# Storing one output tile in five pieces, so that one DMA engine moves fewer rows

## The chip, the cores and the metric

The kernel runs on one core of a Trainium2 chip. A core has TensorE (PE), VectorE (DVE), ScalarE (ACT), GpSimd (POOL) and SyncE (SP), and sixteen DMA engines that move data between HBM and SBUF. The metric is the time of one execution on the device in microseconds (us), as a median of several runs.

## The reference

Batched products of two tensors, over 96 independent pairs of matrices:

```python
batch, n_heads, seq_t, seq_s, channels = 8, 12, 512, 512, 64
x = randn(batch, n_heads, seq_t, channels)   # float32
y = randn(batch, n_heads, seq_s, channels)
out = np.einsum('bhtc,bhsc->bhts', x, y).astype(np.float32)
```

The inputs are 12.6 MB each, the output is 100.7 MB of float32. Four fifths of the traffic is output.

## The kernel before

**Work.** The 96 matrix pairs are taken in 6 groups of 16, loaded as one x tile and one y tile of 128 partitions x 4096 float32 (2 MB) each. The inputs are cast to bf16 and kept (`xk`, `yb`), x is mixed into `xb` by copies, and both are turned on VectorE (`xT`, `yT`). The output is made in 24 tiles, `t` = 0 to 23, of 128 partitions x 8192 float32 (4 MB). A tile is made in four quarters: eight matmuls fill a PSUM tile `pm` (L212), and ScalarE copies it to a quarter of an SBUF slot (L114).

**Slots and stores.** There are three slots of 4 MB, used for loads at first and for output tiles afterwards. When all four quarters of a tile are in its slot, SyncE issues one store (L233): `nc.sync.dma_start(ov[i, z], slots[s])`. The view `ov` has, for one tile, 64 row pairs `p`, two rows `u` in each, and 8192 elements:

```python
ov = out.rearrange("b h t s -> (b h t s)").rearrange(
    "(i u z p n) -> i z p u n", u=2, z=2, p=P // 2, n=K * S
)
```

So one SBUF partition is one row of the store, a contiguous run of 32 KB in HBM. A store has 128 rows. ScalarE refills a slot only when the store that reads it has landed. The last five tiles use slots 2, 1, 0, 2, 1, so that the slot of tile 21 (slot 0) isn't filled again.

**Order.** Everything stands in one order, written out by hand at the end of the function. `emit` records what an instruction reads and writes, and `need` (L72 to L85) puts the semaphore waits that follow from that in front of it, on its engine (L82). A DMA names the semaphore that it raises by 16 (`dma=`). Each engine carries out its own instructions in order. SyncE issues all the DMAs; GpSimd issues none, and has nothing to do after the last y tile is cast. The function ends with SyncE waiting for the last store of each slot:

```python
need("sp", [(f"dma{i}", ticks[f"dma{i}"]) for i in range(0, 2 * BIG, 2)])
```

After it come the barriers of all engines that end the program.

Of the kernel before, what the change touches and what calls it, by code (L numbers as in the profile page):

```python
# [9 lines left out]
def kernel(  # L10
# [22 lines left out]
    nc = tc.nc  # L33
    B, H, T, C = x.shape
    _, _, S, _ = y.shape
    P = 128
# [8 lines left out]
    D = 32  # L45
    BIG = 3
    NT = 2 * NH
    fp32 = mybir.dt.float32
    bf16 = mybir.dt.bfloat16
    u32 = mybir.dt.uint32  # L50
# [3 lines left out]
    xv = x.rearrange("b h t c -> (b h t c)").rearrange("(g p n) -> g p n", p=P, n=R * C)  # L54
    yv = y.rearrange("b h t c -> (b h t c)").rearrange("(g p n) -> g p n", p=P, n=R * C)
    ov = out.rearrange("b h t s -> (b h t s)").rearrange(
        "(i u z p n) -> i z p u n", u=2, z=2, p=P // 2, n=K * S
    )

    sb = ctx.enter_context(tc.tile_pool(name="sb", bufs=1))  # L60
    ps = ctx.enter_context(tc.tile_pool(name="ps", bufs=1, space=bass.MemoryType.PSUM))
    slots = [sb.tile([P, K * S], fp32, name=f"slot{i}") for i in range(BIG)]
    xks = [sb.tile([P, R, C], bf16, name=f"xk{i}") for i in range(NG - 1)]
    ybs = [sb.tile([P, R // 2 * D], u32, name=f"yb{i}") for i in range(2 * NG - 3)]
    xb = sb.tile([P, K * E * D], u32, name="xb")
    xTs = [sb.tile([P, K * D * E], u32, name=f"xT{i}") for i in range(2)]
    yTs = [sb.tile([P, D * R // 2], u32, name=f"yT{i}") for i in range(2)]
    pms = [ps.tile([P, 4, S], fp32, name=f"pm{i}") for i in range(2)]
    engines = {"act": nc.scalar, "dve": nc.vector, "pool": nc.gpsimd, "pe": nc.tensor, "sp": nc.sync}
    sems, ticks, known, snaps, writer, readers = {}, {}, {e: {} for e in engines}, {}, {}, {}  # L70

    def need(name, points):  # L72

        best = {}
        for p, v in points:
            if known[name].get(p, 0) < v:
                best[p] = max(best.get(p, 0), v)
        for p, v in list(best.items()):
            if any(snaps[q, w].get(p, 0) >= v for q, w in best.items() if q != p):
                del best[p]  # L80
        for p, v in best.items():
            engines[name].wait_ge(sems[p], v)  # L82
            known[name][p] = v
            for q, w in snaps[p, v].items():
                known[name][q] = max(known[name].get(q, 0), w)  # L85

    def emit(name, make, reads=(), writes=(), dma=None):

        points = [writer[r] for r in (*reads, *writes) if r in writer]
        points += [v for w in writes for v in readers.get(w, ())]  # L90
        if name == "pool" and name in ticks:
            points.append((name, ticks[name]))
        need(name, points)
        p, step = (name, 1) if dma is None else (f"dma{dma}", 16)
        if p not in sems:
            sems[p] = tc.alloc_semaphore(p)
        make().then_inc(sems[p], step)
        at = (p, ticks.get(p, 0) + step)
        ticks[p] = at[1]
        snaps[at] = {**known[name], p: at[1]}  # L100
        if dma is None:
            snaps[at][name] = at[1]
        for r in reads:
            readers.setdefault(r, []).append(at)
        for w in writes:
            writer[w], readers[w] = at, []
# [14 lines left out]
    def load(n, place):  # L121
        where[n] = place
        s, half = divmod(place, 2)
        emit(
            "sp",
            lambda: nc.sync.dma_start(
                slots[s][:, half * R * C:(half + 1) * R * C], (yv if n % 2 else xv)[n // 2]
            ),
            writes=[("slot", s, 2 * half), ("slot", s, 2 * half + 1)],
            dma=place,  # L130
        )
# [5 lines left out]
    def keep_x(n):  # L137
        src, reads = held(n)
        xk = n // 2 % len(xks)
        copy("act", xks[xk].rearrange("p r c -> p (r c)"), src, reads, [("xk", xk)])  # L140
# [7 lines left out]
    def keep_y(n, half):  # L148
        src, reads = held(n)
        ys = src.rearrange("p (r c) -> p r c", c=C)  # L150
        b = home(n // 2, half)
        yv2 = ybs[b].bitcast(bf16).rearrange("p (j c w) -> p j w c", j=R // 2, w=2)
        for ch in range(2):
            copy(
                in_front[2 * half + ch],
                yv2[ch * 64:(ch + 1) * 64],
                ys[half * 64:(half + 1) * 64, :, ch * D:(ch + 1) * D].rearrange(
                    "p (j w) c -> p j w c", w=2
                ),
                reads,  # L160
                [("yb", b, ch)],
            )

    def mix(i, name, parts=range(4)):

        g, half = divmod(i, 2)
        xk = g % len(xks)
        xv2 = xb.bitcast(bf16).rearrange("p (k e c u) -> p k e c u", k=K, e=E, u=2)
        for part in parts:
            ch, u = divmod(part, 2)  # L170
            lo = half * 64 + u * D
            copy(
                name,
                xv2[part * D:(part + 1) * D, :, :, :, u],
                xks[xk][lo:lo + D, :, ch * D:(ch + 1) * D].rearrange("p (e k) c -> p k e c", k=K),
                [("xk", xk)],
                [("xb", part)],
            )

    def turn_x(i):  # L180
        half = i % 2
        emit(
            "dve",
            lambda: nc.vector.transpose(  # L184
                xTs[half].rearrange("p (k r e) -> p k e r", k=K, e=E),
                xb.rearrange("p (k e c) -> p k e c", k=K, e=E),
            ),
            [("xb", part) for part in range(4)],
            [("xT", half)],
        )  # L190

    def turn_y(i):
        g, half = divmod(i, 2)
        b = home(g, half)
        emit(
            "dve",
            lambda: nc.vector.transpose(  # L197
                yTs[half].rearrange("p (r j) -> p j r", r=D),
                ybs[b].rearrange("p (j c) -> p j c", c=D),
            ),  # L200
            [("yb", b, ch) for ch in range(2)],
            [("yT", half)],
        )
# [24 lines left out]

    def store(t, s):
        i, z = divmod(t, 2)  # L230
        emit(
            "sp",
            lambda: nc.sync.dma_start(ov[i, z], slots[s]),  # L233
            reads=[("slot", s, part) for part in range(4)],
            dma=2 * s,
        )

    with tc.tile_critical():  # L238
        for n in range(2 * BIG):
            load(n, n)  # L240
        emit(
            "dve",
            lambda: nc.vector.memset(xb, 0.0),  # L243
            writes=[("xb", part) for part in range(4)],
        )
        keep_x(0)
        mix(0, "dve")
        turn_x(0)
        keep_y(1, 0)
        keep_y(1, 1)  # L250
        turn_y(0)
        keep_x(2)
        load(6, 2)
        mix(1, "pool", range(1))
        keep_y(3, 0)
        keep_y(3, 1)
        load(7, 3)
        mix(1, "pool", range(1, 3))
        mix(1, "dve", range(3, 4))
        keep_x(4)  # L260
        load(8, 4)
        quarter(0, 0, 0, "act")
        keep_y(5, 0)
        keep_y(5, 1)
        load(9, 5)
        turn_x(1)
        quarter(0, 0, 4, "act")
        keep_x(6)
        load(10, 2)
        quarter(0, 0, 8, "act")  # L270
        keep_y(7, 0)
        keep_y(7, 1)
        load(11, 3)
        turn_y(1)
        quarter(0, 0, 12, "act")
        store(0, 0)
        mix(2, "pool", range(2))
        keep_x(8)
        quarter(1, 2, 0, "act")
        keep_y(9, 0)  # L280
        keep_y(9, 1)
        mix(2, "pool", range(2, 4))
        quarter(1, 2, 4, "act")
        keep_x(10)
        quarter(1, 2, 8, "act")
        quarter(1, 2, 12, "act")
        store(1, 2)
        keep_y(11, 0)
        turn_y(2)
        quarter(2, 1, 0, "act")  # L290
        quarter(2, 1, 4, "act")
        keep_y(11, 1)
        quarter(2, 1, 8, "act")
        quarter(2, 1, 12, "act")
        store(2, 1)
        turn_x(2)
        mix(3, "dve")
        for t in range(3, NT):
            s = (0, 2, 1)[t % 3]
            for k in range(0, K, 4):  # L300
                quarter(t, s, k, "act")
            store(t, s)
            i = t // 2 + 2
            if t % 2 and i < NH:
                turn_y(i)
                turn_x(i)
                if i + 1 < NH:
                    mix(i + 1, "dve")
        need("sp", [(f"dma{i}", ticks[f"dma{i}"]) for i in range(0, 2 * BIG, 2)])


# [28 lines left out]
```

## Time and profile before

| | |
|---|---|
| median of 3 runs | 301.94 us (301.93 to 302.73) |
| profiled execution, its own time | 302.08 us |
| span of the profiled execution, first to last instruction | 300.3 us |
| busy: ACT, DVE, PE, POOL | 71%, 52%, 48%, 14% of the span |
| DMA | 125.95 MB, mean 419 GB/s over the span |
| stores: 24 of 4096 KB | 21.9 us from issue to landing (median) |

The profiled execution's time is 1.78 us more than its span. In the profile, SPq is SyncE's own queue of instructions, L12 is line 12 of the kernel, and all times count from the span's start. A window's DMA share and GB/s count each packet where it starts, with its whole size and length, so that a share can be over 1.

### The profile page before, as it was taken

Reading aid. Unit: us, or ns where it says so; the run is one execution under the profiler, and the core shown is the slowest. Engines: PE = TensorE matmul, PEld = TensorE weight load, DVE = VectorE, ACT = ScalarE, POOL = GpSimd, SP = SyncE. Lnnn points to the kernel's source line nnn. Section 1 sums busy time; section 2 is a strip of 40 time slices with the busy share of each in tenths; the row PEclk is TensorE's granted clock in tenths of the full one; section 3 lists DMA queues with packets and bytes.
Section 4 is the critical chain, followed back from the end, with each engine's and each line's share of the span. In section 5 each row is a group of like instructions: output and inputs, shape, how many; then the busy total and the mean of one; then the engine's idle time right before and its main releaser. Section 6 shows DMA issues by size and latency. Waiting matters only on the chain.

```text
span 300.3 us, 1880 instructions
## 1 busy us (share of the span) xinstructions
PE 144.7 (48%) x768; PEld 46.5 (15%) x768; DVE 156.8 (52%) x78; ACT 212.8 (71%) x109; POOL 41.9 (14%) x17
## 2 busy tenths in 40 slices
PE   0000633454864767655753575558664754664000
PEld 0000210111211222121211121112211211211000
DVE  2399999859494862927709349087192510000000
ACT  1665999999997669776876678667966696669000
POOL 0117977990000000000000000000000000000000
PEclk9999955559598675778779877776679778775555
DMA  7999999999999999999999999999999999999992
GB/s 275 426 436 430 421 419 430 439 421 417 419 445 454 423 417 428 443 445 428 417 428 445 445 423 423 426 445 450 419 423 426 441 450 419 423 426 441 450 423 118
DMA packets 5192, 125.95 MB, mean 419 GB/s; under 512 B 576, under 2 KB 576, under 8 KB 576
## 3 DMA queue, kind: packets, MB, share of 16 engines
q1 hardware_dynamic: 5184, 125.83, 97.9%
q8 instruction: 6, 0.10, 0.1%
q14 instruction: 2, 0.02, 0.0%
HBM read 25.17 MB, written 100.66 MB: 419 GB/s over the span
## 4 chain that ended last, share of the span: by engine, by line
DMA 52%; ACT 19%; DVE 14%; PE 5%; issue 2%; ACTq 0%; SPq 0%
DMA out_dram<-slot 49%; ACT slot L114 16%; DVE yb L116 8%; PE pm L212 5%; DVE xb L116 4%; DMA slot<-in_x_dram 3%; ACT xk L114 2%; DVE yT L197 1%; DVE xT L184 1%; ACT yb L114 1%; ACTq L82 0%; SPq L335 0%; SPq L238 0%
## 5 line engine op out<-in xcount | busy, mean ns | idle before, releaser
L114 ACT ACTIVATE slot<-pm 128x2048 f32<-128x2048 f32 x96 | 175.1, 1877 | 49.3 <-DMA out_dram<-slot 43.3
L212 PE MATMUL pm<-yT,xT 128*64 128x512 bf16 x768 | 144.7, 526 | 130.8 <-ACT slot L114 100.1
L212 PEld LDWEIGHTS pm<-yT,xT 128*64 128x64 bf16 x768 | 46.5, 139 | 228.2 <-ACT slot L114 151.9
L116 DVE COPY xb<-xk 32x2048 bf16<-32x2048 bf16 x41 | 59.5, 1451 | 10.6 <-ACT xk L114 9.3
L197 DVE STREAM_TRANSPOSE yT<-yb 128x1024 uint32<-128x1024 uint32 x12 | 23.6, 1969 | 68.2 <-PE pm L212 68.1
L184 DVE STREAM_TRANSPOSE xT<-xb 128x2048 uint32<-128x2048 uint32 x12 | 46.2, 3848 | 0.1
L116 DVE CAST yb<-slot 64x2048 bf16<-64x2048 f32 x12 | 27.9, 2321 | 4.6 <-DMA slot<-in_y_dram 4.3
L114 ACT ACTIVATE xk<-slot 128x4096 bf16<-128x4096 f32 x6 | 21.7, 3617 | 11.6 <-DMA slot<-in_x_dram 11.6
L116 POOL COPY xb<-xk 32x2048 bf16<-32x2048 bf16 x7 | 22.9, 3272 | 9.7 <-DVE xT L184 9.4
L116 POOL CAST yb<-slot 64x2048 bf16<-64x2048 f32 x6 | 18.8, 3138 | 15.8 <-DMA slot<-in_y_dram 15.3
L114 ACT ACTIVATE yb<-slot 64x2048 bf16<-64x2048 f32 x6 | 14.8, 2474 | 2.8 <-DMA slot<-in_y_dram 2.5
L243 DVE MEMSET xb<- 128x2048 uint32 x1 | 1.8, 1765 | 1.4 <-SPq L238 1.4
L114 ACT ACT_TABLE_LOAD x1 | 1.3, 1283 | 0.9 <-SPq L238 0.9
L324 POOL MEMSET const-float32-0.0<- 128x1 f32 x1 | 0.1, 98 | 0.2 <-issue 0.2
L324 POOL MEMSET const-bfloat16-1.0<- 128x1 bf16 x1 | 0.1, 101 | 0.0
L324 POOL MEMSET const-float32-1.0<- 128x1 f32 x1 | 0.1, 98 | 0.0
L324 POOL MEMSET const-uint8-127<- 128x1 uint8 x1 | 0.1, 98 | 0.0
## 6 DMA issues: line engine op xcount, KB each, us to landing
out_dram<-slot SPq DMA_DIRECT2D x24, 4096.0 KB, 21.9
slot<-in_x_dram SPq DMA_DIRECT2D x6, 2048.0 KB, 14.8
slot<-in_y_dram SPq DMA_DIRECT2D x6, 2048.0 KB, 11.8
```

What stands on the lines that cost most here:

```text
L114: lambda: nc.scalar.activation(dst, src, COPY)
L116: else engines[name].tensor_copy(dst, src),
L184: lambda: nc.vector.transpose(xTs[half].rearrange("p (k r e) -> p k e r", k=K, e=E), xb.rearrange("p (k e c) -> p k e c", k=K, e=E),),
L197: lambda: nc.vector.transpose(yTs[half].rearrange("p (r j) -> p j r", r=D), ybs[b].rearrange("p (j c) -> p j c", c=D),),
L212: last = nc.tensor.matmul(pms[pm][w * 64:(w + 1) * 64, j, :], xT[:, k + j, h, :], yT[:, h * S:(h + 1) * S], start=True, stop=True,)
L243: lambda: nc.vector.memset(xb, 0.0),
L324: nc = _bacc.Bacc("TRN2", target_bir_lowering=False, num_devices=1)
```

## The change

Tile 21, the last but two (`UNEVEN = NT - 3`), is no longer stored by one DMA but by five. SyncE issues a store of rows 0 to 95, two of four rows each (every second row of 118 to 125) and one of the last two rows. GpSimd issues a store of rows 96 to 117, and ahead of it a small load of ten runs of 64 bytes into a new tile `spare` that nothing reads. Each of the six DMAs has a semaphore of its own. At the end SyncE waits for all DMAs but the last store, and ScalarE waits for that one. All other tiles, all loads and all arithmetic are as before.

```diff
+    UNEVEN = NT - 3
...
+    spare = sb.tile([P, 16], fp32, name="spare")
...
     def store(t, s):
         i, z = divmod(t, 2)
+        if t == UNEVEN:
+            return store_unevenly(t, s)
         emit(
...
+    def store_unevenly(t, s):
+
+        i, z = divmod(t, 2)
+        runs = P // 2
+        some = 3 * runs // 4
+        most = some + 11
+        pieces = [("sp", slice(0, 2 * some), ov[i, z][:some])]
+        pieces.append(("pool", slice(2 * some, 2 * most), ov[i, z][some:most]))
+        for u in range(2):
+            pieces.append(("sp", slice(2 * most + u, 2 * runs - 2, 2), ov[i, z][most:runs - 1, u]))
+        pieces.append(("sp", slice(2 * runs - 2, 2 * runs), ov[i, z][runs - 1]))
+        for n, (name, rows, dst) in enumerate(pieces):
+            if name == "pool":
+                emit(
+                    "pool",
+                    lambda: nc.gpsimd.dma_start(spare[:10, :16], xv[0][:15, :16].rearrange("(a b) n -> a b n", b=3)[:, :2]),
+                    writes=["spare"],
+                    dma=100,
+                )
+            emit(
+                name,
+                lambda: engines[name].dma_start(dst, slots[s][rows]),
+                reads=[("slot", s, part) for part in range(4)],
+                dma=101 + n,
+            )
...
-        need("sp", [(f"dma{i}", ticks[f"dma{i}"]) for i in range(0, 2 * BIG, 2)])
+        last = f"dma{2 * s}"
+        need("sp", [(p, n) for p, n in ticks.items() if p.startswith("dma") and p != last])
+        need("act", [(last, ticks[last])])
```

## The prediction

> **What bounds the kernel now.** I read the page first.
>
> ```profile
> DMA  7999999999999999999999999999999999999992
> DMA packets 5192, 125.95 MB, mean 419 GB/s; under 512 B 576, under 2 KB 576, under 8 KB 576
> q1 hardware_dynamic: 5184, 125.83, 97.9%
> q8 instruction: 6, 0.10, 0.1%
> ```
>
> Sixteen DMA engines are busy from the first slice to the last but one, and no compute engine is above 71%. Only the rows left to move count. Next I asked who waits for whom from 245 us on (us in total, times, longest), and what the chain of waits is there (start, us, what).
>
> ```profile
> ACT slot L114 <- DMA out_dram<-slot: 7.0, 3, 2.3
> ```
>
> ```profile
> 247.87 21.94 DMA out_dram<-slot
> ...
> 273.78 3.65 ACT slot L114 x2
> ```
>
> ScalarE waits for a store to free its slot, refills it by 277.4 us and is done; from there the last stores drain. Then I cut the tail into windows (the last two columns are DMA share and GB/s).
>
> ```profile
> 293.00:294.00 1.00, 0.00 (x0) 0.00 (x0) 0.00 (x0) 0.00 (x0) 0.00 (x0) 0.50 1.14 492
> 294.00:295.00 1.00, 0.00 (x0) 0.00 (x0) 0.00 (x0) 0.00 (x0) 0.00 (x0) 0.50 0.69 295
> 295.00:296.00 1.00, 0.00 (x0) 0.00 (x0) 0.00 (x0) 0.00 (x0) 0.00 (x0) 0.50 0.00 0
> 296.00:297.00 1.00, 0.00 (x0) 0.00 (x0) 0.00 (x0) 0.00 (x0) 0.00 (x0) 0.50 0.08 33
> 297.00:298.00 1.00, 0.00 (x0) 0.00 (x0) 0.00 (x0) 0.00 (x0) 0.00 (x0) 0.50 0.08 33
> 298.00:299.00 1.00, 0.00 (x0) 0.00 (x0) 0.00 (x0) 0.00 (x0) 0.00 (x0) 0.50 0.00 0
> ```
>
> 33 GB/s in 1 us is 33 KB: one row starts in 296 to 297 and one in 297 to 298, with nothing beside them. One engine moves its last two rows alone. The trace's packet records (start, length and size of each) say the same to 10 ns. A row takes 1.213 us. Joined end to start they make sixteen chains, and the last rows end at 294.43 to 294.91 (seven engines), 295.37, 295.58, 295.78 to 296.21 (six), and **298.45** (one). The last landing is at 298.92, the span ends at 300.3.
>
> Why that engine is late also stands there. Between 72 and 279 us some 150 rows, about 15 in every 20 us, which is one engine's share, take some 25 ns over 1.213; in sum 3.9 us. The six engines at 295.8 to 296.2 each served one of the six 16 KB instruction fetches of the page (a gap of 0.85 to 0.95 us and a next row longer by 0.37 to 0.41). The records don't number the engines; that the late one is the change's "engine 4" I can't see.
>
> **The change part by part.**
>
> *The rows.* Rows 0 to 95 are six for each of sixteen engines. Rows 96 to 117 by GpSimd are two for each of eleven, 4 + 4 are two for each of four, the last two are one for each of two. If the eleven are 5 to 15, the four 0 to 3 and the two 0 and 1, engine 4 has 6 rows where it had 8, engines 0 and 1 have 9, and the rest 8. The late engine then ends at 298.45 - 2 x 1.213 - 2 x 0.025 = 295.97. Engines 0 and 1, if of the early seven, end at 294.9 + 1.21 = 296.1 at most. What is late next is the six fetch engines, at 296.21. So the end moves by 298.45 - 296.21 = **2.24 us**.
>
> [...]
>
> *Issue.* SyncE issues four DMAs where it issued one. A store's issue takes 0.54 us (median of L233), so at most 3 x 0.54 = 1.6 us more, at 257.7 us. Behind it stands the store of tile 22, issued at 267.7 when ScalarE has filled its slot: 8 us of cover, cost 0. Without cover it would be 1.6 us. GpSimd's last operation ends at 67.7 us; nothing is queued behind its DMAs and nothing but the end waits for them. Its generation has no row here: between SyncE's 0.33 us and GpSimd's own 3.4 us casts. Even 3.4 us is off the path, since rows 96 to 117 have from 258 to 286 us.
>
> *Jumping the queue.* GpSimd's rows come by another queue and may go ahead of tile 20's rows on eleven engines, which can then land 2 x 1.213 = 2.43 us later than 269.8. ScalarE refills that slot for tile 23, so its last store would be issued at 279.9, not 277.4. The first engines need it when tile 22 is moved, about 285.1 (its first landing); a DMA starts moving 1.0 us after its issue (the first load: 0.96 to 1.98). About 4 us of cover are left, cost 0.
>
> *A foreign queue between rows.* The price of a switch is read from the instruction fetches: 16 KB cost an engine 0.88 + 0.40 = 1.28 us, and the 8 KB one at 122.9 us 0.30 + 0.35 = 0.65. Proportional to bytes: 2 x 0.65 - 1.28 leaves 0.02 us for a switch. But at twice a store's time per byte (32 KB in 1.213 is 0.61 for 16 KB). So two rows by GpSimd cost 0 if they run as SyncE's do, and 2 x 1.3 = 2.6 us if they run as fetches do, on engines that would then end last. They are 32 KB rows from SBUF to HBM, as the stores are, so I take 0.
>
> *The last wait.* After its wait, at 298.92, SyncE signals all engines (299.16), they answer (299.20 to 299.25), and the barriers run to 300.3. With ScalarE waiting, SyncE has signalled long before, and ScalarE's answer is the only one missing. Nothing is queued behind ScalarE's wait; its last copy ended at 277.4. The hop is worth 0.2 us at most; a wait that ScalarE takes longer to leave costs as much. Bounds -0.2 to +0.2, value -0.1, since the hop is there in the records.
>
> *Sum.* 302.08 - 2.24 - 0.1 = 299.74 for the profiled execution, which is 0.14 above the median: **299.6 us**, 0.8% less.
>
> **The rivals.** A measurement can tell about 0.3% here, 0.9 us.
>
> *One extra row in the wrong place (0.10).* If engine 0 or 1 is one of the six fetch engines, its ninth row ends at 296.21 + 1.21 = 297.42, and the gain is 1.03 + 0.1: 300.8 us. For it: six of the fifteen others are fetch engines. Against: the seven early ones are the largest group, and the fetches fall on six different engines, which looks like a run of neighbours.
>
> *The rows don't fall as meant (0.12).* If GpSimd's 22 rows are dealt to the first eleven engines, engine 4 keeps 8 rows, and engines 0 and 1 have 11: 294.9 + 3 x 1.21 = 298.5, where the late one is. Or the late engine is another one. Either way 301.9, bounds 301.6 to 302.2: no change.
>
> *The partial tiles are read slower (0.22, the slower side).* All 36 DMAs of the trace have 128 rows, one for each partition. None shows what a transfer from 96 partitions costs. If rows that engines read together share a path, a row takes up to 2 x 1.213. Each doubled row on an engine costs 1.21, so the gain of 2.34 is gone at two of its six; with three the time is 301.94 - 2.34 + 3.64 = 303.2, with all six 306.9. For it: one row at a time takes exactly 1.213 on fifteen engines, which is a hard limit of something, and the packets at the start of the first load, where all engines begin at once, took up to 1.97 us for 16 KB instead of 0.61. Against: the engines drift by up to 3.9 us, three rows, against each other while the stores go on, so which rows are read together changes, and 1.213 doesn't.
>
> [...]
>
> **How the numbers follow.** Forecast 0.56, extra row 0.10, no effect 0.12, partial tiles 0.22. Faster by over 0.3% is the first two, 0.66; within 0.3% is 0.12; slower 0.22. Below, the forecast reaches 299.0: 299.6 less the other 0.1 of the hop and half a row (0.6) that the order of fetches may give. Above, the range takes in the extra row, no effect and the partial tiles up to three doubled rows, 303.2; beyond are some 0.15 above and 0.03 below. The likeliest case alone has 299.0 to 300.2.
>
> **What would show it.** Right: in windows of 1 us from the end back, no stretch with 33 GB/s alone, the last landing 2.3 us earlier against the span's start, the DMA share at 1.0 through 258 to 275 us. Of the steps: the copies of tile 23 still end before 280 us; tile 22's store is issued at about 267.7. Wrong: two single rows are still left at the end (placement), one single row (the extra row), or the DMA rate between 258 and 275 us falls under 420 GB/s and ScalarE's wait for tile 20's slot grows by over 2.4 us (partial tiles).

## The result: slower, and the profile after

The changed kernel takes 310.12 us (median of 6 runs, 309.39 to 310.49), the kernel before 302.23 us beside it (6 runs). The ratio is 1.026, 95% interval 1.0245 to 1.0274: **7.9 us slower**. The profiled execution took 309.94 us, with a span of 308.2. The forecast was 299.6, in a range up to 303.2.

The page after, its GB/s slices and queues:

```profile
GB/s 272 434 432 427 417 432 430 410 430 453 417 425 447 425 436 435 418 459 417 419 451 425 421 447 419 442 438 417 455 419 425 447 421 425 387 291 311 425 379 68
DMA packets 5260, 125.95 MB, mean 409 GB/s; under 512 B 644, under 2 KB 644, under 8 KB 644
q1 hardware_dynamic: 5172, 125.11, 96.6%
q0 software_dynamic: 80, 0.72, 0.8%
```

The bytes are the same. Up to the thirty-fourth slice the rate is as before; then come 387, 291 and 311 GB/s, which is from 262 us on, when tile 21 moves. The page's DMA issues (size, time from issue to landing) show the pieces:

```profile
out_dram<-slot SPq DMA_DIRECT2D x1, 3072.0 KB, 27.3
out_dram<-slot POOLq DMA_DIRECT2D x1, 704.0 KB, 15.3
```

The first piece has three quarters of a tile and needs 27.3 us where a whole tile needs 21.9. The waits from 245 us on and the chain of waits:

```profile
ACT slot L116 <- DMA out_dram<-slot: 11.4, 3, 6.7
```

```profile
247.86 26.35 DMA out_dram<-slot
...
278.18 3.65 ACT slot L116 x2
```

Tile 20's store, already under way, lands 4.4 us later than before (26.35 for 21.94), and ScalarE's longest wait grows from 2.3 to 6.7 us. The same stretch in windows, first of the kernel before, then of the changed one (DMA share and GB/s are the last two columns):

```profile
264.00:279.00 15.00, 7.78 (x40) 2.36 (x36) 0.00 (x0) 10.59 (x6) 0.00 (x0) 0.61 1.01 434
279.00:282.00 3.00, 0.00 (x0) 0.00 (x0) 0.00 (x0) 0.00 (x0) 0.00 (x0) 0.50 1.01 437
```

```profile
264.00:279.00 15.00, 7.08 (x38) 2.33 (x36) 0.00 (x0) 7.77 (x5) 0.00 (x0) 0.61 1.05 324
279.00:282.00 3.00, 0.91 (x6) 0.03 (x2) 0.00 (x0) 2.83 (x2) 0.00 (x0) 0.50 0.79 240
...
303.00:304.00 1.00, 0.00 (x0) 0.00 (x0) 0.00 (x0) 0.00 (x0) 0.00 (x0) 0.50 0.15 66
304.00:305.00 1.00, 0.00 (x0) 0.00 (x0) 0.00 (x0) 0.00 (x0) 0.00 (x0) 0.50 0.15 66
305.00:306.00 1.00, 0.00 (x0) 0.00 (x0) 0.00 (x0) 0.00 (x0) 0.00 (x0) 0.50 0.08 33
```

This is the pair to read: a share of 1.05 with 324 GB/s. The engines aren't idle; the same rows take longer. In the packet records 88 rows that start between 261.9 and 285.1 us take between 1.31 and 5.2 us instead of 1.213. Their excess sums to 94 us, 5.9 us for each engine. The 0.79 of the second stretch isn't idle time either: it comes from counting each row where it starts, and by the records all sixteen engines are at work without a gap from 264 to 297 us. The prediction named these signs for its partial tiles: a rate under 420 GB/s, and ScalarE's wait longer by over 2.4 us (here 4.4). And the end is no longer one late engine but a long tail: the last store's sixteen landings lie between 298.2 and 307.0 us. Their mean moved by 5.95 us (295.86 to 301.81), and the last one's distance from the mean by 2.1 (3.06 to 5.19). Together that is the 8.1 us by which the last landing moved.

### The profile page after: what moved, and what is told of

Read it like the earlier page. It is cut to its first block, busy times and chain, and to the rows that moved or that the text cites. A ratio compares the mean times of both kernels' runs of the same rounds, so it can differ in the third digit from the quotient of the medians.

```text
span 308.2 us, 1888 instructions
## 1 busy us (share of the span) xinstructions
PE 143.1 (46%) x768; PEld 46.2 (15%) x768; DVE 156.3 (51%) x78; ACT 212.7 (69%) x109; POOL 43.6 (14%) x19
## 4 chain that ended last, share of the span: by engine, by line
DMA 52%; ACT 18%; DVE 14%; PE 5%; issue 2%; ACTq 0%; SPq 0%
DMA out_dram<-slot 49%; ACT slot L116 15%; DVE yb L118 8%; PE pm L214 5%; DVE xb L118 4%; DMA slot<-in_x_dram 3%; ACT xk L116 2%; DVE yT L199 1%; DVE xT L186 1%; ACT yb L116 1%; ACTq L84 0%; SPq L367 0%; SPq L268 0%
## 5 line engine op out<-in xcount | busy, mean ns | idle before, releaser
L214 PE MATMUL pm<-yT,xT 128*64 128x512 bf16 x768 | 143.1, 521 | 136.9 <-ACT slot L116 106.2
L118 DVE COPY xb<-xk 32x2048 bf16<-32x2048 bf16 x41 | 58.6, 1430 | 10.5 <-ACT xk L116 9.3
L257 POOL DMA_DIRECT2D spare<-in_x_dram x1 | 1.0, 965 | 0.3 <-POOL yb L118 0.3
## 6 DMA issues: line engine op xcount, KB each, us to landing
out_dram<-slot SPq DMA_DIRECT2D x23, 4096.0 KB, 21.9
out_dram<-slot SPq DMA_DIRECT2D x1, 3072.0 KB, 27.3
```

The costliest lines, as they stand in the source:

```text
L118: else engines[name].tensor_copy(dst, src),
L214: last = nc.tensor.matmul(pms[pm][w * 64:(w + 1) * 64, j, :], xT[:, k + j, h, :], yT[:, h * S:(h + 1) * S], start=True, stop=True,)
L257: lambda: nc.gpsimd.dma_start(spare[:10, :16], xv[0][:15, :16].rearrange("(a b) n -> a b n", b=3)[:, :2]),
```

## Experiments

The main theory from here on is the slower rival of the prediction, called the *crowded path* in the texts below: rows that engines read together from neighbouring partitions share one row's rate. That is a supposition: the paths and groups of partitions in those texts belong to it, and no run shows which partitions would share, or what. Its rivals are GpSimd's queue, the number and size of the pieces, and the wait at the end. All experiments are edits of the kernel before; `pieces` replaces the store of tile 21 as in the change, and unless said otherwise the wait at the end stays with SyncE.

**Two halves by columns, two halves by partitions.**

```diff
+h = K * S // 2
+pieces = [("sp", slots[s][:, q * h:(q + 1) * h], ov[i, z][:, :, q * h:(q + 1) * h]) for q in range(2)]
```

> Tile 21 is stored by two SyncE transfers of all 128 partitions, each with half of the columns (16 KB rows). [...] GpSimd's queue as the cause: no change. Number and size of pieces as the cause (7.9 us for five pieces more): some 1.5 to 2 us slower.

```diff
+pieces = [("sp", slots[s][64 * q:64 * q + 64], ov[i, z][32 * q:32 * q + 32]) for q in range(2)]
```

> Tile 21 is stored by two SyncE transfers of 64 partitions each, all columns, 32 KB rows as before. Crowded path: sixteen engines read 64 rows that lie on half of the paths, each row takes 2 x 1.213 = 2.43 us, the tile 19.4 us instead of 9.7: about 9.7 us slower, 312 us, rows of 2.4 us in the trace. GpSimd's queue: no change, 302.2. Number of pieces: as for the two pieces of columns, at most 2 us slower.

Columns: 302.13 us against 302.09, ratio 0.9999 (0.9989 to 1.0008). Partitions: 310.54 us, ratio 1.0283 (1.0237 to 1.0329), 8.4 us slower. Same bytes, same number of pieces, both by SyncE. The stretch in windows, columns first, then partitions:

```profile
264.00:279.00 15.00, 7.42 (x42) 2.19 (x40) 0.00 (x0) 11.05 (x6) 0.00 (x0) 0.84 0.99 421
```

```profile
264.00:279.00 15.00, 7.65 (x44) 2.35 (x40) 0.00 (x0) 11.19 (x7) 0.00 (x0) 0.84 1.04 281
279.00:282.00 3.00, 0.00 (x0) 0.00 (x0) 0.00 (x0) 0.00 (x0) 0.00 (x0) 0.53 0.97 218
```

218 GB/s at a share of 0.97 is half of the 437 of the kernel before in the same window; the windows of 3 us on either side of it have 229 and 240. In the partition run 111 rows take between 1.32 and 4.44 us, and 42 of them 2.546 to 2.549: 2.1 times one row's time, as if two engines shared one path, with 25.7 GB/s between them where one alone has 27.0. The records don't show which engines meet. By the run of columns, two pieces and rows of half the size cost nothing.

**Rows 0 to 95 and 96 to 127.**

```diff
+pieces = [("sp", slots[s][:96], ov[i, z][:48]), ("sp", slots[s][96:], ov[i, z][48:])]
```

> Tile 21 is stored by two SyncE transfers, rows 0 to 95 and rows 96 to 127; no GpSimd, no small pieces, and the wait at the end stays with SyncE. Crowded path: most of the changed kernel's loss of 7.9 us is there, 306 to 312 us, and rows of 1.8 to 4 us. GpSimd's queue or the small pieces: no change, 302.2 us.

312.31 us, ratio 1.0345 (1.0322 to 1.0368): 10.2 us slower, just above the upper end of what the crowded path gave. The same stretch in a window:

```profile
264.00:279.00 15.00, 7.54 (x40) 2.22 (x36) 0.00 (x0) 9.33 (x6) 0.00 (x0) 0.61 1.07 333
```

Again the share is full and the rate is three quarters; 86 rows take 1.29 to 4.9 us, 89 us over 1.213 in sum. GpSimd, the pieces of four rows and ScalarE's wait aren't needed for the loss.

**The whole tile by GpSimd.**

```diff
+pieces = [("pool", slots[s], ov[i, z])]
```

> Tile 21 is stored by one GpSimd transfer of all 128 rows; everything else goes as before. Crowded path: each engine keeps its own partitions, so 302.2 us within 1 (GpSimd's rows go beside SyncE's, the sum of rows is the same). GpSimd's queue as the cause: several us slower; the changed kernel had two rows of eight there on eleven engines and lost 7.9 us, so four times as many rows would lose well over 8.

302.28 us, ratio 1.0003 (0.9994 to 1.0012). All 128 rows by GpSimd, going beside SyncE's, cost nothing, and 121 of the 128 take 1.213 us exactly. Tile 20's store lands 7.6 us later than in the kernel before (277.4 for 269.8), so GpSimd's rows do go in between its rows, and that is covered too.

**Even and odd partitions.**

```diff
+pieces = [("sp", slots[s][u:128:2], ov[i, z][:, u]) for u in range(2)]
```

> Tile 21 is stored by two SyncE transfers of 64 rows, the even and the odd partitions. Each reaches all groups of partitions, where the two halves of the run before reached half of them each. [...] Crowded path with each engine kept to its own group whatever the transfer: no change, 302.1 us.

302.32 us, ratio 1.0003 (0.9994 to 1.0012). Again two SyncE transfers of 64 rows of 32 KB, and no loss:

```profile
264.00:279.00 15.00, 8.57 (x40) 2.54 (x40) 0.00 (x0) 10.88 (x6) 0.00 (x0) 0.61 0.99 427
```

Against the halves, only which partitions stand in one transfer differs, and with them which rows of HBM it writes: 427 GB/s for 281. So it is neither 64 rows nor two transfers that cost, but 64 *neighbouring* partitions. Whether the rows meet in SBUF, where they are read, or in HBM, where they are written, no run separates. If the crowded path holds, no change here means that each engine keeps to partitions of its own in this transfer too. A loss of 5 to 10 us, which I had also held possible, isn't there. How rows are dealt to the engines, these runs don't show.

**Which engine is late.**

```diff
+for n, k in enumerate((1, 2, 4, 5, 10)):
+    emit("sp", lambda: nc.sync.dma_start(spares[n][:k, :16], xv[0][:3 * k:3, :16]),
+         writes=[("spare", n)], dma=101 + n)
```

> Behind the last store SyncE issues fifteen tiny loads of 2, 3, ... 16 rows of 64 bytes, so that each one's landings show when that many engines have come to the end of their rows. If a transfer of k rows uses the k lowest engines and the late engine is number 4: the loads of 2, 3 and 4 rows land 1 us or more before the end, and from 5 rows on one landing comes at the end, some 2.3 us after all others. If the late engine is another one, the late landing comes first at another count. The time grows by under 1.5 us.

The kernel that ran had five such loads, of 1, 2, 4, 5 and 10 rows, not fifteen. One run, 302.5 us. Their landings, from the records (us; one raise of each semaphore between 279 and 284 us, about when the load is issued, is left out):

```
 1 row : 295.16
 2 rows: 295.34 295.89
 4 rows: 295.22 295.52 295.74 296.06
 5 rows: 295.39 295.69 295.91 296.23 299.06
10 rows: 295.22 295.32 295.57 295.87 296.10 296.31 296.40 296.57 296.75 299.25
```

The late landing first appears with the fifth row, 2.8 us behind the others. The lists fit into each other: 295.16, 295.34, 295.52, 295.69 and 295.87 look like one engine that takes load after load, so a load of more rows seems to use the same engines and further ones. If they are numbered in that order from 0, as in the expectation, engine 4 is the late one and engines 0 to 3 are not. Engine 0 ends its last store at 295.0 us and engine 1 at 295.7, where the last but one of the sixteen ends at 296.83. That the change's own pieces fall on these engines isn't shown by this run.

**The wait at the end alone.**

```diff
-need("sp", [(f"dma{i}", ticks[f"dma{i}"]) for i in range(0, 2 * BIG, 2)])
+last = f"dma{2 * s}"
+need("sp", [(p, n) for p, n in ticks.items() if p.startswith("dma") and p != last])
+need("act", [(last, ticks[last])])
```

> Only the waits at the end change: ScalarE waits for the last store, SyncE for the others; all stores are whole. Crowded path: this part is worth -0.1 us, bounds -0.2 to +0.2, 302.0 against 302.1. If the last wait were behind the loss: several us slower.

301.78 us against 302.25, ratio 0.9989 (0.9980 to 0.9998). From the last landing to the end of the span it is 1.10 us here and 1.16 in the changed kernel, against 1.34 to 1.47 in all profiles in which SyncE waits last. So this part is a gain of 0.2 to 0.3 us against the kernel before (1.38 us).

**Can two rows be moved without the loss?** Less of the tile is put out of place: the first three quarters of the columns stay in one transfer of 128 partitions. On how many engines, and on which, the pieces of this and the next runs fall is assumed as in the prediction; no run shows it.

```diff
+c = 3 * K * S // 4
+pieces = [("sp", slots[s][:, :c], ov[i, z][:, :, :c]), ("pool", slots[s][:88, c:], ov[i, z][:44, :, c:])]
+for p in range(44, 64, 4):
+    for u in range(2):
+        pieces.append(("sp", slots[s][2 * p + u:2 * p + 8:2, c:], ov[i, z][p:p + 4, u, c:]))
```

> The change's shift of rows with less of the tile out of place: three quarters of tile 21's columns go in one transfer of all 128 partitions; of the last quarter (8 KB runs) rows 0 to 87 go by GpSimd on eleven engines after the same small load, rows 88 to 127 by ten SyncE transfers of four rows. Engine 4 moves two rows' worth less, engines 0 to 3 half a row's worth more each, the others as before. By the count of rows, as I predicted: 2.24 us faster, 299.9. Crowded path: the runs still come from the same partitions, so nothing can be gained, and the quarter that is out of place costs about a quarter of the change's 7.9 + 2.2 us: 0 to 3 us slower, 302 to 305. Number of pieces: twelve pieces, well over the 7.9 us of five.

304.54 us, ratio 1.0075 (1.0062 to 1.0088). This one is confounded: the ten pieces took SyncE 1.2 to 3.1 us each to issue, and tile 22's store waited behind them until 278.1 us instead of 267.6. The engines ran dry:

```profile
276.00:279.00 3.00, 0.47 (x4) 0.00 (x0) 0.00 (x0) 2.40 (x2) 0.00 (x0) 0.95 0.40 150
```

So it was done again with few issues, and with half the share:

```diff
+c = 3 * K * S // 4          # second run: 7 * K * S // 8
+pieces = [("sp", slots[s][:, :c], ov[i, z][:, :, :c]),
+          ("pool", slots[s][:120, c:], ov[i, z][:60, :, c:]),
+          ("sp", slots[s][120:128:2, c:], ov[i, z][60:, 0, c:]),
+          ("sp", slots[s][121:128:2, c:], ov[i, z][60:, 1, c:])]
...
+# GpSimd: the change's small load before its piece, one of 24 runs after it
```

> The same two rows' worth off engine 4, in few issues: in the run before, SyncE spent 18 us on ten pieces of four rows and tile 22's store came only at 278 us, so the engines ran dry (150 GB/s from 276 to 279 us). [...] Count of rows, as I predicted: 2.24 us faster, 299.9. Crowded path: the runs still come from the same partitions, engine 4's group has as many bytes as before and 120 runs are read out of place: no gain, 302.1 to 305.

> As the run above with the last eighth of the columns instead of the last quarter, so one row's worth off engine 4. Count of rows: 1.2 us faster, 300.9. Crowded path: no gain, half of the extra time of the run above, 302.1 to 303.6.

As a control, the same quarter by GpSimd in one transfer of all 128 partitions:

```diff
+c = 3 * K * S // 4
+pieces = [("sp", slots[s][:, :c], ov[i, z][:, :, :c]), ("pool", slots[s][:, c:], ov[i, z][:, :, c:])]
```

> Three quarters of tile 21's columns by SyncE, the last quarter by GpSimd, each in a transfer of all 128 partitions on sixteen engines. Crowded path: each engine reads its own partitions, no change, 302.1 within 0.5. If GpSimd's narrower runs (8 KB) cost by themselves: slower, and then a part of the two runs above is theirs.

Quarter: 303.13 us against 302.15, ratio 1.0035 (1.0023 to 1.0048). Eighth: **300.93 us, ratio 0.9965 (0.9952 to 0.9977)**. Control: 302.14 us, ratio 1.0002 (0.9992 to 1.0011). The landings of the last store (us) show two effects side by side:

| | mean of 16 | last but one | last |
|---|---|---|---|
| before | 295.86 | 296.62 | 298.92 |
| eighth | 296.63 | 297.38 | 297.83 |
| quarter | 298.18 | 299.82 | 299.88 |
| the change | 301.81 | 306.23 | 307.00 |

The last engine's lag behind the next shrinks from 2.30 to 0.45 and then to 0.06 us. By the count of rows it would be 1.2 us for each row's worth: the direction is as counted, the two steps (1.85 and 0.39) aren't, and the records don't tell whether it is still the same engine that is last. At the same time all engines get later on average, by 0.77 and 2.32 us; the control, with nothing out of place, has a mean of 295.88. The rows that take longer explain that: their excess sums to some 11 us in the eighth and 33 in the quarter, 0.7 and 2.1 us for each engine. The last landing moves by both together: the mean, and the distance of the last from it (3.06, 1.20 and 1.70 us). My expectation that *nothing* could be gained, because by the theory engine 4's partitions still hold as many bytes, was wrong: the eighth gained 1.2 us. The end of the eighth's span, in windows:

```profile
294.00:295.00 1.00, 0.00 (x0) 0.00 (x0) 0.00 (x0) 0.00 (x0) 0.00 (x0) 0.50 1.06 459
295.00:296.00 1.00, 0.00 (x0) 0.00 (x0) 0.00 (x0) 0.00 (x0) 0.00 (x0) 0.50 0.53 229
296.00:297.00 1.00, 0.00 (x0) 0.00 (x0) 0.00 (x0) 0.00 (x0) 0.00 (x0) 0.50 0.08 33
297.00:298.00 1.00, 0.00 (x0) 0.00 (x0) 0.00 (x0) 0.00 (x0) 0.00 (x0) 0.50 0.00 0
```

One row starts with nothing beside it where there were two.

**Eighth and wait together.** Both edits above in one kernel.

> The two parts that gained, together: the last eighth of tile 21's columns on fifteen engines, and ScalarE waiting for the last store. If the two add (1.2 us and 0.47 us in the runs of each alone): 300.5 us against 302.2. If the exit part was scatter: 301.0. Crowded path without any gain, as I had it before the run of the eighth: 302.1, which that run has already contradicted.

300.95 us against 302.08, ratio 0.9969 (0.9958 to 0.9980). It beats both kernels, by 1.1 us over the one before, and is the same as the eighth alone within the intervals. Its profile has 1.17 us after the last landing, so the wait's 0.2 us is there, but the times of its seven runs (300.4 to 301.6) don't show it. In the run of the wait alone the end of the span accounts for 0.2 to 0.3 of the 0.47 us; that run's interval (some 0.1 to 0.6 us) takes in that gain, so a remainder isn't shown.

## Why the prediction was wrong, step by step

- *What bounds the kernel* was right: one engine's last two rows are the end, and by the tiny loads it is the fifth, engine 4. Engines 0 and 1 have room (they end their last stores at 295.0 and 295.7 us there), though engine 1 isn't of the early seven: with a ninth row it would have ended about 0.1 us behind the next latest.
- *The rows* is the step that failed. It priced every row at 1.213 us, whichever engine reads it and whatever is read beside it. In the trace of before each row is read in a transfer of all 128 partitions, and there every row takes about that. The pieces of neighbouring partitions break it: in the changed kernel 88 rows take 1.31 to 5.2 us, 94 us too much in sum, and 96 + 32 rows in two plain transfers cost 10.2 us without anything else. The count of rows had the right direction (the last engine's lag goes), and is worth 2.3 us at most. The 2.24 us in the forecast's sum rest on where the pieces fall (GpSimd's rows on engines 5 to 15, SyncE's few rows on 0 to 3), which was an assumption of mine, with the small load ahead of GpSimd's store made for it, and which no run shows. What the runs show in its place is the last landing: 1.1 us earlier with an eighth of the tile out of place (297.83 for 298.92), 8.1 us later in the change.
- *The partial tiles* rival named the loss, but had 0.22, and its price was too low. I set a row at twice 1.213 at most, 306.9 us with all six doubled; rows took up to 5.2 us, over four times 1.213, and the measured 310.1 lies above that bound. The argument that spoke against it, that engines drift by three rows and 1.213 doesn't change, was empty: if each engine of a whole transfer reads where no other does, drift can't make them meet.
- *Rows don't fall as meant* doesn't seem to have happened: the tiny loads have engine 4 late, and the eighth, which assumes the same placement, gained 1.2 us. For the pieces themselves no record shows it.
- *Issue*: the three SyncE pieces behind the first took 1.18 to 1.30 us each to issue, not 0.54; all four took 4.4 us where I had 2.2. It isn't that they have few rows: in the run of columns the second transfer, of all 128 partitions, took 1.40 right behind the first. The cover (to 267.6 us) held. In the run with ten pieces it didn't.
- *Jumping the queue*: tile 20's store landed at 274.2 (272.2 at most by my step), tile 23's was issued at 281.9 (279.9). I had counted two rows at 1.213. The cover held all the same: tile 22's first landing came at 288.6, and all engines are at work until 297 us.
- *A foreign queue* costs 0, as taken: a whole tile by GpSimd (1.0003) and a quarter of one (1.0002).
- *The last wait*: -0.2 to -0.3 us, at the end of my bounds or just past it, and not the -0.1.

Why the change lost 7.9 us and the plain 96 + 32 rows 10.2 can be read from their profiles. On average the engines lose nearly the same: the mean of the last store's landings moves by 5.95 us in the change and by 5.46 in the plain split (301.32). The difference is at the end. The last landing is 5.19 us behind the mean in the change, and 7.19 in the plain split, where one engine ends 3.70 us behind the next. So the moved rows may well have helped the last engine, while the crowding cost far more than they could gain.

Open: whether engines meet and which, whether on the side of SBUF or of HBM, and why some 150 rows between 72 and 279 us in the kernel before take some 25 ns over 1.213.

## What to carry to other kernels

When a kernel drains through DMA engines at a fixed time per row (1.213 us here), price a transfer by which partitions it spans too, and not by rows or bytes alone. Here one tile split by columns (302.13 us against 302.09) or by every second partition (302.32 against 302.25) cost nothing, and split into runs of neighbouring partitions it cost 8.4 us (64 + 64) and 10.2 us (96 + 32). The end could be drawn in only with a small share of the tile out of place: an eighth gained 1.2 us, a quarter lost 1.0. And when all rows of a trace have the same duration, that may only mean that the trace never shows the case in which they wouldn't.

## What the runs showed of the hardware

- A store of 128 rows of 32 KB cut into partitions 0 to 63 and 64 to 127 has 42 rows of 2.546 to 2.549 us instead of 1.213, a little worse than half speed, and 218 GB/s instead of 437 from 279 to 282 us; the kernel is 8.4 us slower. Cut into even and odd partitions, or into two halves of the columns, it costs nothing (302.32 us against 302.25, 302.13 against 302.09).
- SyncE issued a whole store in 0.54 us (median in the kernel before). A second transfer right behind a first one took 1.37 to 1.40 us, whether it had 32, 64 or all 128 partitions, and one in a row of ten small ones up to 3.1. At the start of the kernel before, loads right behind another took 0.42 to 0.72.
- GpSimd issued a transfer of 22 to 128 rows in 0.56 to 0.72 us, and the DMA engines took its rows in between SyncE's rows that were queued earlier: with a whole tile by GpSimd, tile 20's store, issued about 10 us ahead of it, landed at 277.4 us instead of 269.8.
- Which engine waits for the last landing matters a little: 1.10 to 1.17 us from there to the end of the span with ScalarE, 1.34 to 1.47 with SyncE.
